# Ten instead of seven down chunks of a float32 MLP with seven block products, and what was rearranged for it

## Chip, cores, metric

One core of a Trainium2 chip. The metric is the device time of one execution in microseconds (us), the median of several runs.

## The reference, cut to what matters

One decoder layer in float32: 256 tokens, model width 2048, 16 heads of 128 (8 of forgetting attention, 8 of dilated attention), then a squared-ReLU MLP of width 8192.

```python
proj = rms_norm(x, norm1_g) @ w_in                 # 2048 x 6152
... two groups of heads, each with an output norm
x = x + mixed @ w_out                              # 2048 x 2048
h = rms_norm(x, norm2_g)
x = x + jnp.square(jax.nn.relu(h @ w_mlp_in)) @ w_mlp_out   # 2048 x 8192, 8192 x 2048
return rms_norm(x, final_norm_g)
```

## The kernel before, in words

**Precision.** Every float32 weight or activation is split into a high and a low part in float32r (ACT copies the high part, `whi`; DVE subtracts it, `wlo`), and a product is three matmuls: high x high, high x low, low x high. A matmul takes 128 weight columns or tokens and streams 256 or 512 columns.

**Tiling.** Each projection is cut into chunks of 512 output columns and each chunk into steps of two k-tiles (2 x 128 rows of the weight). The weights come from HBM in raw tiles of four k-tiles (1 MB, `raw`, L177, on SP's queue); a raw tile serves two steps. A raw tile is free for a new load when its last split has run (`spent`); there are 4 (`wraw`), and `load_more` keeps 4 in use.

**The MLP** runs in four rounds. In each, four up chunks (`u`) give 2048 of the 8192 hidden features, squared, as `hT` (in `big_hi`, `big_lo`), and four down chunks (`d`) add their share to the residual `xs`. A plain step is 24 matmuls of 256 columns: `turned_product` (L414) for up, `product` (L398) for down.

**Seven-product chunks.** Seven down chunks (`seven`, L140) use a scheme of Strassen's kind over 2 x 2 blocks (two token halves, two column halves, two k halves): seven block products instead of eight. It needs sums of weight blocks (`both`, made by DVE at L207, L222, L223 in `split_seven`) and sums of activation blocks (`mix_hi`, `mix_lo`, made by `mix_activations` and `split_mixed`). Such a chunk has four units of one raw tile, and a unit has four steps: "near" (12 matmuls), "first" (6), "odd" (12), "even" (12), in `seven_products` (L460); a plain step of another chunk is put between "odd" and "even". Its four PSUM banks are those of the names "sc" and "tr"; `drain_seven` adds them into `xs` in four parts. Before, the first down chunk of a round runs its units inside the up chunks of the next round, and the second with the steps of the third.

**Order.** The program is written out by hand: `steps` lists the steps in PE's order; the split of a step is called some steps ahead of its products (five step tiles of `whi` and `wlo` are live at a time, and one of `fhi`, `flo` for "first"); other work (drains, norms) is put in by `at(slot, ...)`, two slots a step, and runs on its engine's queue in the order of the calls. `drain_u` reads an up chunk's two PSUM banks (ACT: ReLU, square, high part; DVE: low part), all in the slot that ends the chunk; `mix_activations` and `split_mixed` follow 2 and 4 slots later.

**PSUM.** Eight banks by name: four "acc" for plain chunks, two "sc" and two "tr" for attention and the seven-product chunks, each name a ring of its own.

Of the kernel before, what the change touches and what calls it, by code (L numbers as in the profile page):

```python
# [19 lines left out]
P = 128  # L20
# [4 lines left out]
NH = 8  # L25
# [50 lines left out]
def kernel(  # L76
# [31 lines left out]
    psum = ctx.enter_context(tc.tile_pool(name="psum", bufs=2, space=PSUM))  # L108
# [5 lines left out]


# [24 lines left out]
    seven = {index["d", (r, c)] for r in range(ROUNDS) for c in range(2) if c or r < ROUNDS - 1}  # L140
# [4 lines left out]
    def mixed(ci, unit, behind):  # L145
        b, a, t13, t24 = ((ci, 2 * unit, sub) for sub in ("near", "first", "odd", "even"))
        return [b, a, t13, behind[0], t24] + behind[1:]

    for r in range(ROUNDS):
        for c in range(4):  # L150
            mine = plain(index["u", (r, c)])
            steps += mine[:4] + (mixed(index["d", (r - 1, 0)], c, mine[4:]) if r else mine[4:])
        late = [index["d", (r, c)] for c in range(4)]
        steps += plain(late[3 if r < ROUNDS - 1 else 0])
        for unit in range(4):
            steps += mixed(late[1], unit, plain(late[2])[2 * unit:2 * unit + 2])
        if r == ROUNDS - 1:
            steps += plain(late[3])
# [6 lines left out]
    def load(i):  # L165
        if i >= len(steps) or steps[i][1] % 2 or (steps[i][0], steps[i][1] // 2) in raws:
            return
        ci, s, _ = steps[i]
        _, _, w, r0, c0, cols, _ = chunks[ci]
        t = wraw.tile([P, 4, CW + NH], F32, name="raw")  # L170
# [15 lines left out]
    ring = [0]  # L186
# [9 lines left out]
    late_tiles, late_forms, sums_of = {}, ExitStack(), {}  # L196

    def halves(t):
        return t.rearrange("p k (f c) -> p f k c", f=2)

    def split_seven(i):
        ci, s, sub = steps[i]
        t = raws[ci, s // 2][:, :, :CW]
        half = CW // 2
        if sub == "near":
            both = sums_of[ci, s] = late_tiles["pool"].tile([P, 2, CW], F32, name="both")
            nc.vector.tensor_tensor(halves(both), t[:, :, half:].rearrange("p (f k) c -> p f k c", f=2),  # L207
                                    halves(t[:, :2]), op=ALU.subtract)
        if sub == "first":
            hi, lo = (late_tiles["pool"].tile([P, CW + LINE], F32R, name=n)[:, b:b + CW]  # L210
                      for n, b in (("fhi", NEAR), ("flo", NEAR)))
            src = t[:, :2, :half]
        else:
            hi, lo = part_tiles(i, 2 * CW, NEAR, NEAR)
            src = t[:, 2:] if sub == "near" else sums_of[ci, s]
        hi, lo = (a.rearrange("p (k c) -> p k c", k=2) for a in (hi, lo))
        splits[i] = (hi, lo)
        nc.scalar.activation(hi, src, AF.Copy)  # L218
        nc.vector.tensor_tensor(lo, src, hi.bitcast(F32), op=ALU.subtract)  # L219
        if sub == "odd":  # L220
            a, b = src[:, :, :half], src[:, :, half:]
            nc.vector.tensor_tensor(a, t[:, 2:, half:], a, op=ALU.subtract)  # L222
            nc.vector.tensor_tensor(b, t[:, 2:, :half], a, op=ALU.subtract)  # L223
            spent.add((ci, s // 2))
# [87 lines left out]
    pw = psum.tile([P, 512], F32, name="sc")  # L312
# [6 lines left out]
    def gains(k0, k1):  # L319
        p = psum.tile([P, 512], F32, name="tr")  # L320
# [22 lines left out]
    def to_features(kt0, gain, n=2):  # L343

        p = psum.tile([P, 512], F32, name="tr")
# [4 lines left out]
        for j in range(n):  # L350
            kt = kt0 + j
            split_psum(aT_hi[:, kt, :], aT_lo[:, kt, :], p[:, j * SEQ:(j + 1) * SEQ], gT[:, gain + kt:gain + kt + 1],
                       gain == kt == 0)

# [46 lines left out]
    def turned_product(ci, i, j, kt, kts):  # L401


        if kt == 0:
            accs[ci] = [psum.tile([P, CW], F32, name="acc", bufs=4) for _ in range(2)]
# [12 lines left out]
    def products(i, j):  # L418
# [10 lines left out]
        if kt == 0:  # L429
            accs[ci] = [psum.tile([P, CW], F32, name="acc", bufs=4) for _ in range(TB)]  # L430
# [7 lines left out]
    def seven_products(i, j):  # L438

        ci, s, sub = steps[i]  # L440
        if ci not in accs:
            accs[ci] = [psum.tile([P, CW], F32, name=n) for n in ("sc", "sc", "tr", "tr")]
# [7 lines left out]
            "odd": ((two_, half, m, k2, upper), (four, 0, m, k1, upper)),  # L450
            "even": ((three, half, m, k1, lower), (two_, 0, h, k2, upper)),
# [3 lines left out]
        for n, (bank, c0, (ah, al), k, tokens) in enumerate(todo):  # L455
            acc = bank[:, c0:c0 + half]
            fresh = begin and (bank, sub) in ((one_, "near"), (three, "first"), (two_, "odd"), (four, "odd")) and (
# [5 lines left out]
    def gated_products(ci, i, j, kt, kts, a):  # L463

        if kt == 0:
            accs[ci] = [psum.tile([P, 512], F32, name=n, bufs=k) for n, k in (("acc", 4), ("acc", 4), ("sc", 2))]
# [48 lines left out]
    def gate_sums():  # L515
        m = psum.tile([P, 512], F32, name="tr")
# [19 lines left out]
    def rel_row():  # L536
        p = psum.tile([P, 512], F32, name="sc")
# [52 lines left out]
    def first_norm_rows():  # L590
        d = diagonal.pop()
        square = d[:, SEQ:SEQ + P]
        p = psum.tile([P, 512], F32, name="tr")
# [29 lines left out]
    def scores(g, h):  # L623
# [5 lines left out]
        bank = psum.tile([P, 512], F32, name="sc")  # L629
# [40 lines left out]
    def turn_probs(g, h):  # L670
        pr = probs.pop((g, h))
        p = psum.tile([P, 512], F32, name="tr")
# [9 lines left out]
    def values(g, h):  # L682
# [4 lines left out]
        y = psum.tile([P, 512], F32, name="sc")  # L687
# [19 lines left out]
    def group_norm(kind):  # L707
        p = psum.tile([P, 512], F32, name="tr")
# [8 lines left out]
    rstd2sq = few.tile([P, TB], F32, name="rstd2sq")  # L717
# [10 lines left out]
    def second_norm():  # L728
        nc.vector.tensor_reduce(ssq2s, ssq2, axis=mybir.AxisListType.X, op=ALU.add)
        rsqrt(rstd2, ssq2s, D_MODEL)  # L730
        nc.vector.tensor_tensor(rstd2sq, rstd2, rstd2, op=ALU.mult)

# [3 lines left out]
    def drain_u(r, c, ci):  # L736

        hT_hi, hT_lo = squares()
        acc = accs.pop(ci)
        kept[c] = []  # L740
        for half in range(2):
            h = two.tile([P, CW], F32, name="nat")
            nc.scalar.activation(h, acc[half], AF.Relu)
            nc.scalar.activation(h, h, AF.Square)
            k0 = 4 * c + 2 * half
            split_psum(
                hT_hi[:, k0:k0 + 2, :].rearrange("p k s -> p (k s)"),
                hT_lo[:, k0:k0 + 2, :].rearrange("p k s -> p (k s)"), h,
            )
            kept[c].append(h.rearrange("p (k s) -> p k s", k=2))  # L750

    kept = {}

    def mix_activations(c):

        a, b = kept[c]
        (a11, a21), (a12, a22) = ((x[:, :, :P], x[:, :, P:]) for x in (a, b))
        nc.vector.tensor_tensor(a22, a21, a22, op=ALU.add)
        nc.vector.tensor_tensor(a21, a11, a21, op=ALU.subtract)
        nc.vector.tensor_tensor(a11, a22, a11, op=ALU.subtract)  # L760
        nc.vector.tensor_tensor(a12, a12, a11, op=ALU.subtract)

    def split_mixed(c):
        for half, x in enumerate(kept.pop(c)):
            k0 = 4 * c + 2 * half
            split_psum(mix_hi[:, k0:k0 + 2, :], mix_lo[:, k0:k0 + 2, :], x)
# [12 lines left out]
    def drain_d(r, c, ci):  # L779
        for t in range(TB):  # L780
            add_down(accs[ci][t], t, slice(c * CW, (c + 1) * CW), c if r == ROUNDS - 1 else None)

    def drain_seven(r, c, ci, part):
# [4 lines left out]
        def add(t, cs, acc):  # L788
            xc = xs[:, t, cs]
            if len(acc.shape) > 2:  # L790
# [244 lines left out]
```

## Time and profile before

| | |
|---|---|
| median of 3 runs | 1082.13 us (1082.01 to 1082.14) |
| the profiled execution: its time, its span | 1082.24 us, 1080.4 us |
| PE busy | 1069.3 us (99%), 8693 matmuls |
| DVE, ACT, POOL busy | 800.2 (74%), 604.4 (56%), 27.9 us (3%) |
| mean granted TensorE clock | 0.997 |
| loads of the MLP weights | 128 of 1 MB, 5.5 and 5.0 us from issue to landing |
| HBM read and written over the span | 193 GB/s |

PE is TensorE's matmuls, PEld its weight loads, DVE VectorE, ACT ScalarE, POOL GpSimd, SP the engine whose queue issues most DMAs. A group row reads: line, engine, operation, out<-in, shapes, count | busy us, mean ns of one | idle us of the engine just before them, and what released it. A timeline row reads: start us, duration us, engine, line, operation, out<-in, count, [idle before <-releaser].

### The profile page before, as it was taken

How to read it: one execution, taken by the hardware profiler on the slowest of the kernel's cores; microseconds unless marked ns; L12 is line 12 of the kernel's file. 1: busy time of each engine (PE TensorE's matmuls, PEld its weight loads, DVE VectorE, ACT ScalarE, POOL GpSimd, SP SyncE). 2: the span in 40 equal slices, each digit the busy share in tenths (PEclk: the TensorE clock that was granted, in tenths of full speed). 3: DMA queues.
4: the chain of work that ended last, by engine and by line, in shares of the span. 5: the costliest groups of instructions: out<-in, count | busy, mean ns of one | idle time of the engine just before them, and what ended most of it. 6: DMA issues, size and time to landing. Idle time of an engine off the chain costs nothing.

```text
span 1080.4 us, 20584 instructions
## 1 busy us (share of the span) xinstructions
PE 1069.3 (99%) x8693; PEld 1037.8 (96%) x8693; DVE 800.2 (74%) x1076; ACT 604.4 (56%) x821; POOL 27.9 (3%) x42
## 2 busy tenths in 40 slices
PE   9999999999999999999999999999999999999996
PEld 7999899998988899999999999999999999999996
DVE  6666756667577666559887788987778886778886
ACT  6555535545455555565556665556665555666561
POOL 0010200000001000000000000000000000000000
PEclk9999999999999999999999999999999999999998
DMA  9765464555554557654676654665656566556652
GB/s 323 238 226 165 157 197 154 195 159 172 201 172 163 185 166 221 201 196 161 219 217 194 202 209 166 201 208 178 199 202 223 196 197 193 196 195 217 211 198 79
DMA packets 105401, 209.38 MB, mean 194 GB/s; under 512 B 3971, under 2 KB 5084, under 8 KB 105180
## 3 DMA queue, kind: packets, MB, share of 16 engines
q1 hardware_dynamic: 104412, 206.59, 57.8%
q8 instruction: 68, 1.11, 0.4%
q0 software_dynamic: 304, 1.06, 0.3%
q10 hardware_dynamic: 592, 0.40, 0.1%
q14 instruction: 25, 0.20, 0.1%
HBM read 205.93 MB, written 2.11 MB: 193 GB/s over the span
## 4 chain that ended last, share of the span: by engine, by line
PE 99%; DMA 0%; DVE 0%; POOL 0%; ACTq 0%; DVEq 0%; issue 0%
PE acc L414 48%; PE acc L398 34%; PE sc L460 7%; PE tr L460 5%; PE tr L349 1%; PE sc L690 1%; PE sc L398 1%; PE sc L646 1%; PE tr L674 0%; DMA xs<-in_x_dram 0%; PE sc L642 0%; PE sc L692 0%; PE sc L636 0%; PE sc L640 0%; DVE xs L858 0%; PE sc L694 0%
## 5 line engine op out<-in xcount | busy, mean ns | idle before, releaser
L253 DVE TENSOR_TENSOR wlo<-raw,whi 128x1024 fp32r<-128x1024 f32 (+2 forms) x327 | 394.3, 1221 | 151.6 <-ACT whi L252 148.4
L252 ACT ACTIVATE whi<-raw 128x1024 fp32r<-128x1024 f32 (+2 forms) x328 | 339.5, 1050 | 218.5 <-PE acc L414 129.8
L414 PE MATMUL acc<-aT_hi,whi 128*128 128x256 f32 x1536 | 425.4, 277 | 0.0
L414 PE MATMUL acc<-aT_hi,wlo 128*128 128x256 f32 x1536 | 423.8, 276 | 0.0
L414 PE MATMUL acc<-aT_lo,whi 128*128 128x256 f32 x1536 | 423.7, 276 | 0.0
L414 PEld LDWEIGHTS acc<-aT_hi,whi 128*128 128x128 f32 x1536 | 288.2, 188 | 1.1 <-issue 0.9
L414 PEld LDWEIGHTS acc<-aT_lo,whi 128*128 128x128 f32 x1536 | 288.2, 188 | 0.1
L414 PEld LDWEIGHTS acc<-aT_hi,wlo 128*128 128x128 f32 x1536 | 288.1, 188 | 0.1
L398 PE MATMUL acc<-whi,big_hi 128*128 128x256 f32 (+1 forms) x680 | 202.8, 298 | 0.0
L398 PE MATMUL acc<-wlo,big_hi 128*128 128x256 f32 (+1 forms) x680 | 202.3, 297 | 0.0
L398 PE MATMUL acc<-whi,big_lo 128*128 128x256 f32 (+1 forms) x680 | 202.2, 297 | 0.0
L398 PEld LDWEIGHTS acc<-wlo,big_hi 128*128 128x128 f32 x680 | 127.6, 188 | 5.1
L398 PEld LDWEIGHTS acc<-whi,big_lo 128*128 128x128 f32 x680 | 127.7, 188 | 4.7
L398 PEld LDWEIGHTS acc<-whi,big_hi 128*128 128x128 f32 x680 | 127.6, 188 | 4.7
L218 ACT ACTIVATE whi<-both 128x1024 fp32r<-128x1024 f32 x56 | 59.8, 1067 | 55.1 <-DVE both L223 26.2
L219 DVE TENSOR_TENSOR wlo<-both,whi 128x1024 fp32r<-128x1024 f32 x56 | 68.3, 1220 | 6.7 <-ACT whi L218 5.8
L336 DVE TENSOR_TENSOR big_lo<-nat,big_hi 128x512 fp32r<-128x512 f32 x32 | 22.2, 693 | 43.7 <-ACT big_hi L335 43.7
L398 PE MATMUL acc<-whi,aT_hi 128*128 128x512 f32 (+1 forms) x144 | 51.7, 359 | 0.0
L398 PE MATMUL acc<-whi,aT_lo 128*128 128x512 f32 (+1 forms) x144 | 51.0, 354 | 0.0
L398 PE MATMUL acc<-wlo,aT_hi 128*128 128x512 f32 (+1 forms) x144 | 51.0, 354 | 0.0
L335 ACT ACTIVATE mix_hi<-nat 128x512 fp32r<-128x512 f32 x32 | 18.5, 625 | 29.9 <-DVE nat L760 29.9
L218 ACT ACTIVATE whi<-raw 128x1024 fp32r<-128x1024 f32 x28 | 29.6, 1058 | 9.4 <-PE acc L398 6.4
(212 smaller groups left out, 1356.7 us busy)
## 6 DMA issues: line engine op xcount, KB each, us to landing
raw<-in_w_mlp_in_dram SPq DMA_DIRECT2D x64, 1024.0 KB, 5.5
raw<-in_w_mlp_out_dram SPq DMA_DIRECT2D x64, 1024.0 KB, 5.0
raw<-in_w_in_dram SPq DMA_DIRECT2D x42, 1024.0 KB, 5.2
raw<-in_w_out_dram SPq DMA_DIRECT2D x16, 1024.0 KB, 5.0
raw<-in_w_in_dram SPq DMA_DIRECT2D x4, 1040.0 KB, 8.7
xs<-in_x_dram SPq DMA_DIRECT2D x3, 512.0 KB, 9.5
raw<-in_w_in_dram SPq DMA_DIRECT2D x2, 512.0 KB, 5.3
big_lo<-rel_d POOLq DMA_DIRECT2D x1, 1024.0 KB, 7.8
```

The costliest lines, as they stand in the source:

```text
L218: nc.scalar.activation(hi, src, AF.Copy)
L219: nc.vector.tensor_tensor(lo, src, hi.bitcast(F32), op=ALU.subtract)
L252: nc.scalar.activation(hi[:, :, c:c + step], t[:, :, c:c + step], AF.Copy)
L253: nc.vector.tensor_tensor(lo, t, hi.bitcast(F32), op=ALU.subtract)
L335: nc.scalar.activation(hi, src, AF.Copy)
L336: nc.vector.tensor_tensor(lo, src, hi.bitcast(F32), op=ALU.subtract)
L349: nc.tensor.transpose(p[:, j * SEQ + t * P:j * SEQ + (t + 1) * P], xs[:, t, c:c + P], ident)
L398: nc.tensor.matmul(acc, x, part[:, j, cols], start=go and n == 0, stop=end and n == 2, skip_group_check=True)
L414: nc.tensor.matmul(acc, w[:, j, b * P:(b + 1) * P], a[:, kt, :], start=kt == 0 and b % 2 == 0 and n == 0, stop=kt == kts - 1 and n == 2, s ...
L460: nc.tensor.matmul(acc, a[:, k, tokens], w[:, j, n * half:(n + 1) * half], start=fresh and x == 0, stop=s == KT // 2 - 2 and j == 1 and x ...
L646: nc.tensor.matmul(s[:, c0:c1], q[:, a, h, rows], k[:, b, h, keys], start=False, stop=n == 2, skip_group_check=True)
L690: nc.tensor.matmul(y[:, :SEQ], v[:, 0, dims], p[:, m, :SEQ], start=n == 0, stop=False, skip_group_check=True)
```

## The change

- **More seven-product chunks.** Ten of the 16 down chunks: the first three (A, B, C) of rounds 0 to 2, and the second of the last round.
- **Their order.** Units are dealt over the whole round by patterns: `2 A0 3 A1 1` means two plain steps, unit 0 of A, three plain steps, unit 1 of A, one plain step; each unit takes one more plain step inside. A runs in the last up chunk and the fourth down chunk, B from there into the next round's first up chunk, C in its second and third. The drain of a round's first up chunk (from the second round on) is put 14 slots later, since C's first unit still reads the features that it overwrites.
- **Unit sums.** The tile `both` is gone: sums are made in place in the raw tile. The first is made by a DMA from POOL's queue that adds half of the first two k-tiles of the weight (256 KB, rows of 1 KB) onto the other half of the raw tile; three adds or subtracts of 512 elements a partition follow on DVE. Signs in `mix_activations`, `seven_products` and `drain_seven` change to match (a negated scale `rstd2neg`).
- **Tiles.** A fifth raw tile (`raw5`). "first" takes one of the five step tiles, half used. A raw tile of a unit is spent at "even" instead of "odd".
- **PSUM.** One ring of eight banks in the MLP: the bank that has been free longest is taken (`take_bank`), and a drain gives its banks back as it reads them (`give_back`); a seven-product chunk takes a bank when a product first needs it.
- **Drains.** `drain_u`, its low parts (`rest_u`), the mixes and their splits are dealt out over ten slots, half by half; `drain_seven` runs in four consecutive slots.

```diff
-    seven = {index["d", (r, c)] for r in range(ROUNDS) for c in range(2) if c or r < ROUNDS - 1}
+    seven = [index["d", (r, c)] for r in range(ROUNDS) for c in range(3) if r < ROUNDS - 1 or c == 1]
...
+    def weave(ci, r, pattern):
+        rest = plain(ci)
+        for token in pattern.split():
+            if token.isdigit():
+                steps.extend(rest[:int(token)])
+                del rest[:int(token)]
+                continue
+            of = index["d", (r - 1 if token.endswith("-") else r, "ABC".index(token[0]))]
+            b, a, t13, t24 = ((of, 2 * int(token[1]), sub) for sub in ("near", "first", "odd", "even"))
+            steps.extend([b, a, t13] + rest[:1] + [t24])
+            del rest[:1]
+
+    behind = ["2 B1- 1 B2- 1 B3- 1", "2 C0- 2 C1- 2", "2 C2- 2 C3- 2"]
+    begun = [["8", "8", "8", "2 A0 3 A1 1"]] + [behind + ["2 A0 3 A1 1"]] * 2 + [behind + ["8"]]
     for r in range(ROUNDS):
...
+        for c, pattern in enumerate(begun[r]):
+            weave(index["u", (r, c)], r, pattern)
+        if r < ROUNDS - 1:
+            weave(index["d", (r, 3)], r, "1 A2 2 A3 2 B0")
+        else:
+            weave(index["d", (r, 0)], r, "2 B0 2 B1 2")
+            weave(index["d", (r, 2)], r, "1 B2 2 B3 3")
+            steps += plain(index["d", (r, 3)])
...
+        if steps[i][2]:
+            nc.gpsimd.dma_start(t[:, :2, CW // 2:CW], src[:, :2, :CW // 2], accum_op=ALU.add)
...
-            if len(raws) - len(spent) >= 4:
+            if len(raws) - len(spent) >= (5 if late_tiles else 4):
...
     def split_seven(i):
...
+        left, right = slice(0, half), slice(half, CW)
+        size = half if sub == "first" else CW
+        hi, lo = (a.rearrange("p (k c) -> p k c", k=2) for a in part_tiles(i, 2 * size, NEAR, NEAR))
+        splits[i] = (hi, lo)
+        x = {"near": t[:, 2:], "first": t[:, :2, left]}.get(sub, t[:, :, right])
...
+        nc.scalar.activation(hi, x, AF.Copy)
+        nc.vector.tensor_tensor(lo, x, hi.bitcast(F32), op=ALU.subtract)
+        first, second = t[:, :2, right], t[:, 2:, right]
         if sub == "near":
+            nc.vector.tensor_tensor(second, second, first, op=ALU.add)
+        elif sub == "odd":
+            nc.vector.tensor_tensor(first, second, t[:, :2, left], op=ALU.subtract)
+            nc.vector.tensor_tensor(second, second, t[:, 2:, left], op=ALU.add)
+        elif sub == "even":
             spent.add((ci, s // 2))
...
+        if s == j == 0:
+            held = accs.setdefault(ci, [None] * 4)
+            for n in {"near": (0,), "first": (2,), "odd": (1,), "even": (3,)}[sub]:
+                held[n] = take_bank("sc")
...
+    def drain_u(c, ci, half):
+        h = two.tile([P, CW], F32, name="nat")
+        kept[c] = kept[c] + [h] if half else [h]
+        nc.scalar.activation(h, accs[ci][half], AF.Relu)
+        give_back(accs[ci][half])
+        nc.scalar.activation(h, h, AF.Square)
+        nc.scalar.activation(both_squares(c, half)[0], h, AF.Copy)
+
+    def rest_u(c, half):
+        hi, lo = both_squares(c, half)
+        nc.vector.tensor_tensor(lo, kept[c][half], hi.bitcast(F32), op=ALU.subtract)
...
     def drain_seven(r, c, ci, part):
...
         if part == 0:
...
+            nc.scalar.activation(s[:, 1], four[:, left], AF.Copy)
             nc.scalar.activation(s[:, 0], three[:, left], AF.Copy)
             add(0, cs, one_)
+            give_back(four, one_)
         elif part == 1:
+            nc.vector.tensor_tensor(rest, rest, late_tiles["copies"][:, 0], op=ALU.subtract)
             add(0, cs, three)
             add(0, slice(cs.start + half, cs.stop), two_[:, right])
         elif part == 2:
+            nc.vector.tensor_tensor(rest, rest, late_tiles["copies"][:, 1], op=ALU.subtract)
             add(1, cs, two_)
+            give_back(two_)
         else:
-            add(1, cs, rest[:, None, :].to_broadcast([P, 2, half]))
+            add(1, slice(cs.start, cs.start + half), rest, rstd2neg)
+            add(1, slice(cs.start + half, cs.stop), rest)
+            give_back(three)
             accs.pop(ci)
...
         elif what == "u":
-            at(e, drain_u, *key, ci)
-            at(e + 2, mix_activations, key[1])
-            at(e + 4, split_mixed, key[1])
+            if key[0] and not key[1]:
+                e += 14
+            for half in range(2):
+                at(e + half, drain_u, key[1], ci, half)
+                at(e + 1 + half, rest_u, key[1], half)
+                at(e + 3 + half, mix_activations, key[1], half)
+                at(e + 6 + half, split_mixed, key[1], half, False)
+                at(e + 8 + half, split_mixed, key[1], half, True)
         elif ci in seven:
             for part in range(4):
-                at(e + 1 + 2 * part, drain_seven, *key, ci, part)
+                at(e + 2 + part, drain_seven, *key, ci, part)
...
     def free_tiles(i):
-        live = [steps[n][2] for n in range(i, done + 2) if not (steps[n][0] == len(chunks) - 1 and steps[n][1] < 3)]
-        return len([n for n in live if n != "first"]) <= 5 and live.count("first") <= 1
+        return len([n for n in range(i, done + 2) if steps[n][0] < len(chunks) - 1 or steps[n][1] > 2]) <= 5
...
     for i in range(final):
         if i == mlp_start:
+            unused_banks += turns["acc"][:2] + turns["sc"] + turns["tr"] + turns["acc"][2:]
...
+            late5.tile([P, 4, CW], F32, name="raw5")
```

More of the change, by code (lines that the diff above doesn't have):

```diff
@@ L113, with take_bank, give_back @@
     ctx.enter_context(tc.manual_schedule())
+    turns = {"acc": [0, 1, 2, 3], "sc": [4, 5], "tr": [6, 7]}
+    unused_banks, number = [], {}
+    def take_bank(kind):
+        if late_tiles:
+            n = unused_banks.pop(0)
+        else:
+            n = turns[kind].pop(0)
+            turns[kind].append(n)
+        t = psum.tile([P, CW], F32, name=f"bank{n}")
+        number[id(t)] = n
+        return t
+    def give_back(*tiles):
+        if late_tiles:
+            unused_banks.extend(number[id(t)] for t in tiles)
     chunks = []
@@ L204, in split_seven @@
         half = CW // 2
-        if sub == "near":
[L206 to L223, printed above, removed]
+        left, right = slice(0, half), slice(half, CW)
[3 more added lines that the diff above has]
+        x = {"near": t[:, 2:], "first": t[:, :2, left]}.get(sub, t[:, :, right])
+        if sub in ("odd", "even"):
+            hi, lo = (a.rearrange("p k (f c) -> p f k c", f=2) for a in (hi, lo))
+            x = x.rearrange("p (f k) c -> p f k c", f=2)
+        nc.scalar.activation(hi, x, AF.Copy)
+        nc.vector.tensor_tensor(lo, x, hi.bitcast(F32), op=ALU.subtract)
+        first, second = t[:, :2, right], t[:, 2:, right]
+        if sub == "near":
+            nc.vector.tensor_tensor(second, second, first, op=ALU.add)
[3 more added lines that the diff above has]
+        elif sub == "even":
             spent.add((ci, s // 2))
@@ L404, in turned_product @@
         if kt == 0:
-            accs[ci] = [psum.tile([P, CW], F32, name="acc", bufs=4) for _ in range(2)]
+            accs[ci] = [take_bank("acc") for _ in range(2)]
         hi, lo = splits[i]
@@ L429, in products @@
         if kt == 0:
-            accs[ci] = [psum.tile([P, CW], F32, name="acc", bufs=4) for _ in range(TB)]
+            accs[ci] = [take_bank("acc") for _ in range(TB)]
         go, end = kt == 0, kt == kts - 1
@@ L449, in seven_products @@
             "first": ((three, 0, h, k1, lower),),
-            "odd": ((two_, half, m, k2, upper), (four, 0, m, k1, upper)),
-            "even": ((three, half, m, k1, lower), (two_, 0, h, k2, upper)),
+            "odd": ((two_, half, m, k2, upper), (three, half, m, k1, lower)),
+            "even": ((four, 0, m, k1, upper), (two_, 0, h, k2, upper)),
         }[sub]
@@ L456, in seven_products @@
             acc = bank[:, c0:c0 + half]
-            fresh = begin and (bank, sub) in ((one_, "near"), (three, "first"), (two_, "odd"), (four, "odd")) and (
+            fresh = begin and (bank, sub) in ((one_, "near"), (three, "first"), (two_, "odd"), (four, "even")) and (
                 bank is not one_ or n == 0)
@@ L731, in second_norm @@
         nc.vector.tensor_tensor(rstd2sq, rstd2, rstd2, op=ALU.mult)
+        nc.vector.tensor_scalar(rstd2neg, rstd2sq, -1.0, None, op0=ALU.mult)
     def squares():
         return rows_at(big_hi, BIG_HI), rows_at(big_lo, BIG_LO)
[L736 to L750, printed above, removed]
@@ L768, with split_mixed @@
+    def split_mixed(c, half, rest):
+        k = slice(4 * c + 2 * half, 4 * c + 2 * half + 2)
+        hi, lo, x = mix_hi[:, k, :], mix_lo[:, k, :], kept[c][half].rearrange("p (k s) -> p k s", k=2)
+        if rest:
+            nc.vector.tensor_tensor(lo, x, hi.bitcast(F32), op=ALU.subtract)
+        else:
+            nc.scalar.activation(hi, x, AF.Copy)
     ssq3 = few.tile([P, TB, 5], F32, name="ssq3")
```

94 lines of the change are left out of this document (42 added, 52 removed).

## Prediction

> **What bounds the kernel now.** I read the page first (busy shares, clock, chain), then the windows of the MLP, then the groups, then the timelines of the tightest places.
>
> ```profile
> span 1080.4 us, 20584 instructions
> PE 1069.3 (99%) x8693; PEld 1037.8 (96%) x8693; DVE 800.2 (74%) x1076; ACT 604.4 (56%) x821; POOL 27.9 (3%) x42
> PE 99%; DMA 0%; DVE 0%; POOL 0%; ACTq 0%; DVEq 0%; issue 0%
> ```
>
> PE is never without work, and the chain of waits is PE from end to end. The MLP, where all of the change lies, in the view by windows (PE, PEld, DVE, ACT, POOL busy with their counts; clock; DMA share; GB/s):
>
> ```profile
> 394.20:1071.60 677.40, 677.40 (x5978) 677.23 (x5976) 533.45 (x620) 392.87 (x474) 2.03 (x3) 1.00 0.60 196
> 831.90:872.70 40.80, 40.80 (x363) 40.80 (x362) 35.55 (x38) 22.02 (x23) 0.00 (x0) 1.00 0.61 204
> ```
>
> 677.40 us over 5978 matmuls is 0.1133 us each, at full clock, with no gap. The timeline of PE shows the same step from start to start, across the border between a unit of a seven-product chunk (L460) and a plain step (L414), 0.12 and 0.11 us:
>
> ```profile
> 806.15 0.28 PE L460 MATMUL tr<-whi,mix_lo 128*128 128x256 f32 x1
> 806.27 0.28 PE L414 MATMUL acc<-aT_hi,whi 128*128 128x256 f32 x1
> 806.38 0.28 PE L414 MATMUL acc<-aT_lo,whi 128*128 128x256 f32 x1
> ```
>
> So a matmul fewer is worth 0.1133 us, and the only question is whether its feeders (DVE, ACT, loads) keep up.
>
> **What the change removes from PE.** A plain down chunk is 16 k-tiles x 2 token halves x 2 column halves x 3 terms = 192 matmuls of 256 columns. A seven-product chunk is 4 units x (12 + 6 + 12 + 12) = 168, of the same kind. Seven such chunks become ten: 3 x 24 = 72 matmuls fewer (5976 to 5904), 72 x 0.1133 = 8.16 us. Nothing else is taken from PE or added to it; the sign changes and the new order of steps leave the matmul count alone.
>
> **What it adds on DVE.** Prices, from the groups (mean ns) of the MLP window:
>
> ```profile
> L253 DVE TENSOR_TENSOR wlo<-raw,whi 128x1024 fp32r<-128x1024 f32 x194 | 234.3, 1222 | 85.0 <-ACT whi L252 83.0
> L207 DVE TENSOR_TENSOR both<-raw 128x1024 f32<-128x1024 f32 x28 | 34.1, 1217 | 0.0
> L219 DVE TENSOR_TENSOR flo<-raw,fhi 128x512 fp32r<-128x512 f32 x28 | 19.1, 683 | 0.0
> L222 DVE TENSOR_TENSOR both<-raw,both 128x512 f32<-128x512 f32 x28 | 19.4, 692 | 1.0
> L336 DVE TENSOR_TENSOR big_lo<-nat,big_hi 128x512 fp32r<-128x512 f32 x32 | 22.2, 693 | 43.7 <-ACT big_hi L335 43.7
> L792 DVE SCALAR_TENSOR_TENSOR xs<-tr,rstd2sq,xs 128x512 f32<-128x512 f32 x14 | 10.4, 745 | 0.0
> L792 DVE SCALAR_TENSOR_TENSOR xs<-sc,rstd2sq,xs 128x256 f32<-128x256 f32 x7 | 3.4, 484 | 0.2
> L801 DVE TENSOR_TENSOR tr<-tr,copies 128x256 f32<-128x256 f32 x7 | 3.0, 425 | 0.0
> L758 DVE TENSOR_TENSOR nat<-nat 128x256 f32<-128x256 f32 x16 | 6.7, 417 | 0.0
> ```
>
> A unit before: one 1217 (the sums), three low parts of 1222, one of 683, two of 692: 6.95 us. After: the 1217 goes, the first sum is the transfer's, and three 512-wide sums in place stand instead of two: 3.67 + 0.68 + 2.08 = 6.43 us. Twelve units more take 77.2 and give back 24 plain splits of 1.222 (29.3); 28 units save 0.52 each (14.7); three seven-chunk drains instead of plain ones: a new one is two of 425, three of 745, one of 742-745 less (the last add of 512 becomes two of 484), in all 2 x 0.425 + 3 x 0.745 + 3 x 0.484 = 4.54 against two of 0.745, so +3.05 each (9.1), and the seven old ones +0.22 each (1.6). Sum: +43.9, DVE 533 to 577 of 669 us, from 79% to 86%. ACT's part of it:
>
> ```profile
> L252 ACT ACTIVATE whi<-raw 128x1024 fp32r<-128x1024 f32 x315 | 328.4, 1058 | 211.3 <-PE acc L414 129.8 <-PE acc L398 56.7 <-PE tr L460 9.0
> L218 ACT ACTIVATE fhi<-raw 128x512 fp32r<-128x512 f32 x28 | 17.3, 616 | 0.0
> L799 ACT ACTIVATE copies<-tr 128x256 f32<-128x256 f32 x7 | 2.6, 369 | 0.0
> ```
>
> 12 x (3 x 1.06 + 0.62) - 24 x 1.06 and three pairs of copies, 22 us more: 415, 62%. It does not bound.
>
> A mean hides the densest stretch. That is the last down chunk of rounds 0 to 2: 8 plain steps with three units (A2, A3, B0), 318 matmuls, 36.0 us of PE. Durations overstate DVE there, because its instructions overlap; one unit of before in the timeline gives the true steps:
>
> ```profile
> 842.76 1.22 DVE L207 TENSOR_TENSOR both<-raw 128x1024 f32<-128x1024 f32 x1
> 843.90 1.22 DVE L219 TENSOR_TENSOR wlo<-raw,whi 128x1024 fp32r<-128x1024 f32 x1
> 845.03 0.69 DVE L219 TENSOR_TENSOR flo<-raw,fhi 128x512 fp32r<-128x512 f32 x1
> 845.63 1.22 DVE L219 TENSOR_TENSOR wlo<-both,whi 128x1024 fp32r<-128x1024 f32 x1
> 846.89 0.69 DVE L222 TENSOR_TENSOR both<-raw,both 128x512 f32<-128x512 f32 x1
> 847.61 0.69 DVE L223 TENSOR_TENSOR both<-raw,both 128x512 f32<-128x512 f32 x1
> 848.22 1.22 DVE L253 TENSOR_TENSOR wlo<-raw,whi 128x1024 fp32r<-128x1024 f32 x1
> 849.52 1.23 DVE L219 TENSOR_TENSOR wlo<-both,whi 128x1024 fp32r<-128x1024 f32 x1
> ```
>
> 1.14 for 1024 wide, 0.60 for 512, 0.72 where the next reads the result. A unit of after is 3 x 1.14 + 0.60 + 0.61 + 0.72 + 0.61 = 5.96. The stretch: 8 x 1.14 + 3 x 5.96 = 27.0, the drain of the up chunk before it some 4.0 (four low parts of 0.60, four half-width mixes of about 0.4), the drain of A some 4.3: 35.3 of 36.0 us, 98%. Before, the densest was the 831.90 window, 35.55 of 40.80 (87%). The stretches on either side are at about 88% (31.3 us of PE) and 77% (36.0), so a lag is not carried on.
>
> **Does the lag reach PE?** What counts is when a low part ends against the start of its matmuls. Before, the tightest place comes after each up drain, where DVE waits in order for the chain on ACT:
>
> ```profile
> 791.51 0.60 ACT L743 ACTIVATE nat<-acc 128x512 f32<-128x512 f32 x1 [1.09 <-PE acc L414]
> 793.34 0.58 ACT L743 ACTIVATE nat<-acc 128x512 f32<-128x512 f32 x1
> 795.16 1.05 ACT L218 ACTIVATE whi<-raw 128x1024 fp32r<-128x1024 f32 x1
> 804.27 1.22 DVE L253 TENSOR_TENSOR wlo<-raw,whi 128x1024 fp32r<-128x1024 f32 x1
> ```
>
> That low part ends at 805.49 and its matmuls start at 806.27 (quoted above): 0.78 us to spare, nine times in the kernel, and no wait of PE. After, the drain is dealt out: 1.83 us of ACT a half, with a split between the halves. I count from PE's start of the first step behind an up chunk (time 0), with four steps split ahead. In the dense stretch: ACT ends half 0 at 1.4, the high part of the plain step inside A2 at 2.4, half 1 at 4.2, that of A2's "even" at 5.2; DVE then ends its low part at 6.4 (PE wants it at 8.84), the mixes at 8.2, the next plain low part at 9.3 (PE: 10.2), the one behind it at 10.6 (12.92). Least room 0.9 us. In the last up chunk of rounds 1 and 2, where the drain of C comes on top (0.8 us of it after time 0): "odd" with its two sums ends at 4.95, the up chunk's low parts at 7.0, the plain step's low part at 8.1 (PE: 8.84), the mixes at 9.9, "even" at 11.0 (11.56). Least room 0.5 us. So I put the waits at 0 to 0.3 us in all. If ACT and DVE together run 1.3 us later than counted, these five places (three and two) lose 0.4 to 0.8 us each: 2 to 4 us, the upper end.
>
> The banks: by the new order a bank is taken at the earliest 66 matmuls (7.5 us) after the drain that frees it is called (C0's "odd", a new round's first up chunk). DVE ran within 6 us of its calls in the places worked out above, so cost 0, with about 1 us a place if that cover is gone. The steps behind a drain are on DVE's own queue, counted already.
>
> **The transfer on POOL's queue.** It is new: 40 of 256 KB, in rows of 1 KB, adding in SBUF, each waiting on POOL for its own load; POOL has nothing else in the MLP until the end (2.03 us of work). DVE's first in-place sum waits for it, and everything behind that on DVE. The nearest rows are the two POOL transfers of the attention part (12 KB and 1 MB, the latter in 1 KB rows) and the loads:
>
> ```profile
> L544 POOL DMA_DIRECT2D big_lo<-rel_d x1: 977/977/977, 69.2 to 69.2; - x1
> DMA to landing us min/median/max: 1.9/4.9/7.8
> big_lo<-rel_d POOLq DMA_DIRECT2D x1, 1024.0 KB, 7.8
> raw<-in_w_mlp_out_dram SPq DMA_DIRECT2D x64, 1024.0 KB, 5.0
> ```
>
> 1.9 for 12 KB and 7.8 for 1 MB: between them 3.3 us for 256 KB, which I take, being nearest in size and run length. Below, 1.9; above, 7.8, or 15.6 if reading and adding to the target doubled it. Room: in a dense stretch two raw tiles (one unit, two plain steps: 90 matmuls) last 10.2 us, so five raw tiles last 25.5; a tile is in use from its first to its last split, 842.76 to 850.75 above, 8.0 us; 17.5 are left for load and transfer, 5.0 + 3.3 = 8.3. In the order's tightest place the load is called 144 matmuls (16.3 us) ahead of the split, and about 2.5 are lost until the tile is free: 13.8. Cost 0, also at 7.8. DMA carries 10.5 MB more over a share of 0.60: 0.03 to 0.06 more. The fifth raw tile is what pays for it, since now the tile is kept until "even".
>
> **Sum.** The profiled execution took 1082.24 us (span 1080.4); 1082.24 - 8.16 = 1074.08. The median of the runs shown, 1082.13, lies 0.11 below. With 0.1 for waits: 1074.1 us.
>
> **Rivals.** (1) *DVE is late in the dense stretches.* For it: 98% and 0.5 to 0.9 us of room; against: before ran with 0.78 and lost nothing, and the lag is worked off in the next stretch. With 0.48 us lost in each of the five places, 2.4 us: 1076.5. (2) *The transfer is late, the other side.* Each unit then waits for it on DVE, and loads wait for tiles: the cycle of five tiles is 8.0 + 5.0 + transfer instead of 25.5. At 15.6 it is 28.6, 12% more in the six densest stretches (216 us): +26 us, 1100. It eats the gain from 3.8% of a cycle, 1.0 us over, a transfer of 13.5 us on. For it: no adding transfer is in the trace; against: 1 MB took 7.8. (3) *POOL's issue is held up by a busy DVE.* DVE's longest run without a gap is about the 8.0 us above; then 5.0 + 3.3 + 8.0 = 16.3, inside 17.5 but 2.5 over the tightest 13.8; a lag of 2.5 us on DVE, where the order leaves 0.5 to 0.9, costs 1 to 2 us in each of the three densest stretches: about 5 us, 1079. The L544 issue took 0.98 us with little DVE work around it, which leaves it open. [...] (4) *The gain does not show at all*, as waits of PE replace it: 1082; this needs 1.6 us lost in each of the five places, against 0.5 to 0.9 us of room in the count.
>
> **How the numbers follow.** Forecast 0.70, rival 1 0.14, rival 2 0.08, rival 3 0.05, rival 4 0.03. The range goes from 1073.6 (no wait, and the sum against the median, with the scatter of the runs) to 1077.5 (rival 1); rivals 2 to 4 are left out. A difference under 0.2% (2.2 us) is about what this measurement cannot tell from none. Faster by more: forecast, rival 1, part of rival 3: 0.88; same 0.03; slower 0.09.
>
> **What would show it.** Right: 5904 matmuls in the MLP over about 669 us at 0.1133 us, PE at 99%, DVE busy near 577 us there, POOL transfers landing in 2 to 8 us, the gap ahead of DVE's in-place sums near zero. Wrong: PE idle released by DVE low parts in the last down chunk of rounds 0 to 2 or in the last up chunk of rounds 1 and 2 (rival 1); DVE idle released by the transfer, in every unit (2) or with a long POOL issue (3); PE waiting for a drain at a unit's first matmul (banks).

## Result and the profile after

| | before | after |
|---|---|---|
| time, median (range) | 1082.07 us (1081.90 to 1082.14) | 1074.74 us (1073.73 to 1075.67), 4 runs |
| ratio, 95% interval | | 0.9926 [0.9914, 0.9938] |
| the profiled execution: time, span | 1082.24, 1080.4 us | 1075.40, 1073.6 us |
| MLP's matmuls, first to last start | 5976 in 677.16 us | 5904 in 669.26 us |
| first matmul of the MLP starts at | 394.19 us | 395.45 us |

The page of after (busy time and share of each engine; the DMA queue of POOL; issues, size and median time to landing):

```profile
span 1073.6 us, 20818 instructions
PE 1062.7 (99%) x8621; PEld 1030.9 (96%) x8621; DVE 840.9 (78%) x1162; ACT 618.0 (58%) x851; POOL 76.1 (7%) x82
q0 software_dynamic: 11184, 11.55, 6.8%
raw<-in_w_mlp_out_dram SPq DMA_DIRECT2D x64, 1024.0 KB, 6.8
raw<-in_w_mlp_out_dram POOLq DMA_DIRECT2D x40, 256.0 KB, 4.6
```

PE has 72 matmuls fewer (8693 to 8621) and stays at 99%. The view by windows of after: the MLP, and the last down chunk of round 2 with its three units, which the prediction named as the densest stretch (PE, PEld, DVE, ACT, POOL busy; clock; DMA share; GB/s):

```profile
395.40:1064.90 669.50, 669.50 (x5906) 669.28 (x5905) 574.09 (x706) 406.75 (x504) 50.24 (x43) 1.00 0.68 212
823.90:859.94 36.04, 36.04 (x321) 36.04 (x319) 33.38 (x43) 23.55 (x30) 4.78 (x4) 1.00 0.74 219
```

No gap of PE is shown, though DVE went from 533 to 574 us. What DVE waited for at the first in-place sum (L250: us in all, times, longest), and how long the adding transfers (L213) took:

```profile
DVE raw L250 <- DMA raw<-in_w_mlp_out_dram: 2.9, 2, 1.6
...
DMA to landing us min/median/max: 4.2/4.6/9.0
```

38 of the 40 transfers had landed when DVE came to them, by 7.1 us at the median over all 40. Two had not, and PE lost a little behind each: 0.05 us in the last up chunk of round 2 (at 804.4 us), and 0.21 in the final round (at 1017.9), where a low part came 0.14 us after PE had reached its step.

One run of `twice3` (1306.29 us) fell in a slower state of the chip and is left out of the median given for it below.

**The profiled execution's account.** Predicted 1074.08; measured 1075.40. Of the 1.32 us, 0.27 are in the MLP: 669.26 against 5904 steps of 0.11333 us (669.00), 0.26 of them at these two places. 1.26 lie before the MLP, in the first ten microseconds: the trace's clock records have PE at full clock from 5.69 us in before, from 9.14 us in after. The rest (-0.21) is in the tail and around the span. The clock's change is seen in the timeline, where three idle products of 512 columns (L316 in before, L347 in after) took 0.81 and 1.49 us:

```profile
6.54 0.81 PE L316 MATMUL sc<-nat 128*128 128x512 bf16 x3
```

```profile
6.75 1.49 PE L347 MATMUL bank<-nat 128*128 128x512 bf16 x3
```

From matmul 300 on (40.87 and 42.13 us) the two executions run in step until the MLP. The times of both kernels fall into two such groups (below), so this is not the change's doing.

### The profile page after: what moved, and what is told of

The parts are those of the page before. It is cut to its first block, busy times and chain, and to the rows that moved or that the text cites. A ratio compares the mean times of both kernels' runs of the same rounds, so it can differ in the third digit from the quotient of the medians.

```text
span 1073.6 us, 20818 instructions
## 1 busy us (share of the span) xinstructions
PE 1062.7 (99%) x8621; PEld 1030.9 (96%) x8621; DVE 840.9 (78%) x1162; ACT 618.0 (58%) x851; POOL 76.1 (7%) x82
## 3 DMA queue, kind: packets, MB, share of 16 engines
q1 hardware_dynamic: 104412, 206.59, 57.3%
## 4 chain that ended last, share of the span: by engine, by line
PE 99%; DMA 0%; DVE 0%; POOL 0%; ACTq 0%; DVEq 0%; issue 0%
PE bank L446 49%; PE bank L430 29%; PE bank L494 18%; PE bank L380 1%; PE bank L724 1%; PE bank L680 1%; PE bank L708 0%; DMA xs<-in_x_dram 0%; PE bank L676 0%; PE bank L726 0%; PE bank L670 0%; PE bank L674 0%; PE bank L347 0%; DVE xs L902 0%; PE bank L728 0%; PE bank L572 0%
## 5 line engine op out<-in xcount | busy, mean ns | idle before, releaser
L446 PE MATMUL bank<-aT_hi,whi 128*128 128x256 f32 x1536 | 426.1, 278 | 0.0
L446 PE MATMUL bank<-aT_lo,whi 128*128 128x256 f32 x1536 | 423.8, 276 | 0.0
L446 PE MATMUL bank<-aT_hi,wlo 128*128 128x256 f32 x1536 | 423.7, 276 | 0.0
L446 PEld LDWEIGHTS bank<-aT_hi,whi 128*128 128x128 f32 x1536 | 288.7, 188 | 1.2 <-issue 0.6
L446 PEld LDWEIGHTS bank<-aT_lo,whi 128*128 128x128 f32 x1536 | 288.4, 188 | 0.1
L446 PEld LDWEIGHTS bank<-aT_hi,wlo 128*128 128x128 f32 x1536 | 288.1, 188 | 0.0
L246 ACT ACTIVATE whi<-raw 128x1024 fp32r<-128x1024 f32 (+1 forms) x160 | 150.9, 951 | 149.8 <-PE bank L446 55.4
L247 DVE TENSOR_TENSOR wlo<-raw,whi 128x1024 fp32r<-128x1024 f32 (+1 forms) x160 | 173.7, 1087 | 47.9 <-ACT whi L246 46.6
L430 PE MATMUL bank<-whi,big_hi 128*128 128x256 f32 (+1 forms) x488 | 149.8, 307 | 0.0
L430 PE MATMUL bank<-wlo,big_hi 128*128 128x256 f32 (+1 forms) x488 | 149.4, 306 | 0.0
L213 POOL DMA_DIRECT2D raw<-in_w_mlp_out_dram x40 | 48.2, 1205 | 559.2 <-DMA raw<-in_w_mlp_out_dram 242.5
```

The costliest lines, as they stand in the source:

```text
L213: nc.gpsimd.dma_start(t[:, :2, CW // 2:CW], src[:, :2, :CW // 2], accum_op=ALU.add)
L246: nc.scalar.activation(hi, x, AF.Copy)
L247: nc.vector.tensor_tensor(lo, x, hi.bitcast(F32), op=ALU.subtract)
L430: nc.tensor.matmul(acc, x, part[:, j, cols], start=go and n == 0, stop=end and n == 2, skip_group_check=True)
L446: nc.tensor.matmul(acc, w[:, j, b * P:(b + 1) * P], a[:, kt, :], start=kt == 0 and b % 2 == 0 and n == 0, stop=kt == kts - 1 and n == 2, s ...
```

## Experiments

Two theories stood against each other. A, the prediction's: PE never waits, the gain is the count of matmuls, and the order leaves DVE just enough room. B: the gain is partly eaten, and parts of the change are ballast or cost something. The runs on the start have theories of their own under these letters. The table gives the MLP's matmuls from first to last start, and from the window over them PE's idle time (its length less PE busy) and by how much PE busy exceeds 0.11333 us for each matmul in it (a lower clock, and short stops inside a recorded matmul; the window counts some matmuls that lie only partly in it, which makes this column about 0.25 us too small).

| kernel | time us | ratio to before | MLP us | PE idle | PE busy over its steps |
|---|---|---|---|---|---|
| after, unaltered (`again`) | 1074.28 | 0.9917 [0.9904, 0.9931] | 669.00 | 0 | 0 |
| nine chunks (`nine`) | 1076.60 | 0.9950 [0.9937, 0.9962] | 671.72 | 0 | 0 |
| before, drains dealt (`before_dealt`) | 1082.10 | 0.9999 [0.9990, 1.0008] | 677.16 | 0 | 0 |
| first sum on DVE (`sum_dve`) | 1075.25 | 0.9931 [0.9919, 0.9944] | 670.24 | 0.3 | 0.7 |
| banks apart (`fixed`) | 1079.24 | 0.9972 [0.9962, 0.9982] | 674.03 | 4.2 | 0.6 |
| drains in bulk (`bulk`) | 1089.35 | 1.0051 [1.0037, 1.0065] | 682.82 | 8.4 | 5.2 |
| four raw tiles (`raw4`) | 1115.03 | 1.0307 [1.0281, 1.0334] | 713.77 | 26.6 | 17.9 |
| transfer twice (`twice2`) | 1148.73 | 1.0605 [1.0548, 1.0663] | 750.15 | 49.1 | 31.8 |
| transfer three times (`twice3`) | 1250.73 | 1.155 [1.1521, 1.158] | 840.5 | 106.8 | 64.5 |

### The changed kernel again, and its start

`again` and `again2` are the changed kernel unaltered.

> The changed kernel once more, unaltered. Theory A (the gain is the 72 matmuls, and what lies between 1074.0 and the slower executions is the clock of the first 10 us): times fall in two groups, about 1073.7 to 1074.1 and 1075.3 to 1075.7, and this execution's profile shows the start of its group: the three idle products between the first transposes and the first weights take 0.8 us (full clock) or 1.5 us (half), and the MLP's 5904 matmuls take 669.1 to 669.5 us in both. Rival B (the spread is made in the MLP, by transfers that land late): the start is the same in all, and the MLP's matmuls take 669.3 us or over 670.5 us.

> The changed kernel unaltered, for its spread. Theory A (the moment at which the granted clock becomes full differs from run to run and sets two groups that lie 1.3 to 1.5 us apart): times at 1073.7 to 1074.6 and at 1075.3 to 1075.7, MLP's matmuls 669.0 to 669.3 us. Theory B (the two groups come of waits in the MLP): the slower profile has over 670 us there.

The MLP's view by windows in `again`:

```profile
394.40:1063.60 669.20, 669.20 (x5907) 669.15 (x5905) 574.30 (x706) 406.80 (x504) 50.24 (x43) 1.00 0.68 212
```

669.00 us from first to last start: 8.160 less than before, 72 x 0.11333 = 8.160. In `again2` it was 669.47. Of all 13 runs of the changed kernel, eight lie at 1073.7 to 1074.6 and five at 1075.4 to 1076.3 (two of these, in `again2`, above the 1075.7 that had been expected). In their three profiles PE's clock is full from 4.28 us (1074.17 us), 9.14 (1075.40) and 10.27 (1076.26, with 0.47 us of it lost in the MLP, at the same two places as in after). Before has the same pair of groups in the later runs, 1081.8 to 1082.7 and 1082.9 to 1084.0 with one run at 1085.3, though with only 0.3 us between the groups, and its variant with dealt drains shows the late start in its profile (10.15 us, 1083.80). The medians of the two groups lie 1.5 us apart in both kernels (1074.12 and 1075.67, 1081.92 and 1083.45).

More idle products ahead of the first real one, run twice:

```diff
-WARM, WARM2 = 8, 3
+WARM, WARM2 = 12, 3
```

> The changed kernel with 12 instead of 8 idle products ahead of the first transposes (1.7 us more of idle PE work at half clock, of which 1.1 us lie in a wait). Theory A: the full clock is there at 6 us in every execution, so all times are 1073.8 to 1074.4, with no second group. Rival B: two groups 1.6 us apart as before. Rival C (the moment of the clock does not depend on the work before it): two groups as well, with the idle products at 1.5 us in the slower.

> The changed kernel with 12 idle products ahead of the first real one instead of 8, a second time. Theory A (four idle products more let the clock become full before the real products begin): one group, all runs at or below 1074.6 us. Theory C (the moment is set by something that runs free of the kernel): two groups as in the changed kernel, some runs at 1075 us or above.

1074.17 us (0.9916 [0.9902, 0.9930]) and 1073.89 us (0.9923 [0.9911, 0.9936]); nine runs from 1073.67 to 1074.75, none in the upper group, where the unaltered kernel had five of 13. One run is 0.15 us above the line that theory A drew. The clock was full from 7.09 and 4.99 us, the MLP took 669.00 us in both. The timeline of `warm12b` shows PE waiting 0.23 us before the second transpose, the first that has to wait for its input, where after waited 1.07 us:

```profile
5.64 0.27 PE L380 MATMUL bank<-ident,xs 128*128 128x128 f32 x1
6.15 0.55 PE L380 MATMUL bank<-ident,xs 128*128 128x128 f32 x3 [0.23 <-DMA xs<-in_x_dram]
```

So the idle products fill a wait for the input and cost nothing, and the late start did not occur. By chance alone all five late runs of these 22 would fall on the unaltered kernel about once in 20 times, and beside `warm12` that kernel had no late run either (`again`), so that twelve products prevent the late start is likely but not shown; the gain, 0.4 us between the medians over all runs, is below what this measurement tells from none. What sets the moment, which goes from 4.28 to 10.27 us for one and the same kernel, is not shown.

### Nine chunks instead of ten

```diff
-if r < ROUNDS - 1 or c == 1]
+if (r < ROUNDS - 1 or c == 1) and (r, c) != (2, 2)]
-    ... + [behind + ["8"]]
+    ... + [behind[:1] + ["8"] * 3]
...
+            if r == 2:
+                steps += plain(index["d", (r, 2)])
...
-            if key[0] and not key[1]:
+            if key[0] in (1, 2) and not key[1]:
```

> Nine seven-product chunks of 16 instead of ten: the third down chunk of round 2 is made plain again (24 matmuls more, 8 dealt steps with their four transfers fewer). Theory A (PE never waits, so the time goes by the count of matmuls): 24 x 0.1133 = 2.72 us more than the change, MLP's matmuls 669.0 + 2.72 = 671.7 us, 1076.8 us in all, and the transfers left land in about 4.6 us as before. Theory B (the tenth chunk already costs waits, or its raw tiles and loads hold up others): less than 2.0 us more, at the least nothing (1074.1).

```profile
394.00:1065.80 671.80, 671.80 (x5930) 671.80 (x5929) 557.82 (x680) 401.67 (x494) 45.42 (x39) 1.00 0.68 210
```

671.72 us, 2.72 more than `again`: the 24 matmuls, to the hundredth. The tenth chunk is paid in full, its 16.5 us of DVE included (574.3 against 557.8). Theory B is out for the count of chunks.

### Drains: dealt out, or in bulk

```diff
             for half in range(2):
-                at(e + half, drain_u, key[1], ci, half)
-                at(e + 1 + half, rest_u, key[1], half)
-                at(e + 3 + half, mix_activations, key[1], half)
-                at(e + 6 + half, split_mixed, key[1], half, False)
-                at(e + 8 + half, split_mixed, key[1], half, True)
+                at(e, drain_u, key[1], ci, half)
+                at(e, rest_u, key[1], half)
+            ... mixes at e + 2, their splits at e + 4, both halves
```

> The up drains as before the change: both halves with their low parts in the slot that ends the chunk, the mixes two slots later, their splits four slots later; all else as changed. DVE then waits in its queue for ACT's chain (1.8 and 1.1 us in the trace of before) at each of 16 drains. Theory A (room of 0.0 to 0.9 us behind each drain of rounds 0 to 3 that units follow): 1 to 2.5 us lost at each of about ten drains, 1084 to 1099. Rival E (dealing them out was worth little, as before the change 0.78 us were left with the drain in one slot): under 2 us, 1074 to 1076.

`bulk` is slower than the kernel before. What PE waited for in its MLP:

```profile
PE bank L446 <- DVE wlo L284: 6.8, 9, 1.9
PE bank L430 <- DVE wlo L284: 1.5, 4, 0.8
```

```profile
395.80:1078.70 682.90, 674.55 (x5906) 671.99 (x5904) 574.36 (x706) 406.02 (x504) 50.23 (x43) 1.00 0.67 208
```

DVE's busy time is that of after (574); only its order differs. The two largest losses, 1.8 and 3.8 us, lie in the last up chunk of rounds 1 and 2, where the drain of C comes on top of the up drain. Of the 3.8 us, 1.6 come after PE's stop of 1.90 us, at half the clock:

```profile
812.31:815.72 3.41, 3.41 (x19) 3.41 (x18) 3.41 (x4) 2.98 (x4) 0.00 (x0) 0.50 0.35 77
```

In the kernel before the same dealing out (the up drains of after in before.py's order, nothing else) does nothing, as theory A had it:

> The kernel before with one part of the change alone: its up drains dealt out over ten places instead of four pieces of work in bulk; the seven chunks of before, their order and their banks stay. Theory A (before had room everywhere, so dealing out has nothing to shorten): no difference, 1082.1 us, MLP's matmuls 677.16 us. Theory B (dealing out has a gain or a price of its own, more instructions on DVE and ACT): at least 0.5 us off that, to either side.

```profile
395.80:1073.10 677.30, 677.30 (x5979) 677.30 (x5977) 535.01 (x620) 391.61 (x474) 2.03 (x3) 1.00 0.60 196
```

677.16 us again, ratio 0.9999. Dealing out is worth 13.8 us with ten chunks (1.6 of them this half clock) and nothing with seven.

### The first sum on DVE

```diff
-            nc.gpsimd.dma_start(t[:, :2, CW // 2:CW], src[:, :2, :CW // 2], accum_op=ALU.add)
...
+            nc.vector.tensor_tensor(first, first, t[:, :2, left], op=ALU.add)
```

> The first unit sum is made by DVE (one 512-wide add more a unit) instead of by the transfer. It adds 40 x 0.60 = 24 us to DVE, and the densest stretch goes from 98% to 37.1 of 36.0 us. Theory A (DVE's room was down to 0.0 to 0.9 us in about twenty places, so it is at its limit): the MLP gets 3 to 10 us longer, 1077 to 1084. Rival D (a lag of 0.6 us a unit is worked off before PE sees it; the transfer buys nothing): 1074 to 1075, as the changed kernel.

```profile
395.70:1066.00 670.30, 670.01 (x5906) 669.42 (x5904) 596.74 (x746) 404.56 (x504) 2.03 (x3) 1.00 0.58 196
```

DVE rises to 596.7 us, 89%, and the MLP loses 1.24 us: three stalls of 0.41 us, one behind each densest stretch, at the third plain step of the next round's first up chunk, which is none of the five places that the prediction named. There DVE has no gap and is simply late: PE's step waits from 869.92 for the low part that ends at 869.01 + 1.22 = 870.23 us.

```profile
869.01 1.22 DVE L283 TENSOR_TENSOR wlo<-raw,whi 128x1024 fp32r<-128x1024 f32 x1
...
869.92 0.28 PE L445 MATMUL bank<-aT_lo,whi 128*128 128x256 f32 x1
870.29 0.39 PE L445 MATMUL bank<-aT_hi,wlo 128*128 128x256 f32 x1
```

Theory A had expected more than twice this. The transfer takes 22 us of work from DVE and buys 1.2 us, since most of these 22 lay in slack.

### Banks

Plain chunks and seven-product chunks each get four of the eight banks, in place of the bank that has been free longest:

```diff
-            n = unused_banks.pop(0)
+            n = next(b for b in unused_banks if (b < 4) == (kind == "acc"))
+            unused_banks.remove(n)
```

> Banks are not taken by age from all eight: plain chunks keep four of their own, seven-product chunks the other four. Where one such chunk follows another, its first bank is then one whose drain was called only three slots (about 4 us) before, instead of 7.5 us and more. Theory A (DVE runs 4 to 6 us behind its calls behind a drain): 0.5 to 2 us of PE waiting at each of eight such places, 1077 to 1090. Rival (the drains run in time): 1074 to 1075.

PE's waits in `fixed`, one of the three in the timelines of DVE and PE, and the MLP by windows:

```profile
PE bank L495 <- DVE xs L833: 4.2, 3, 1.6
```

```profile
857.05 0.74 DVE L833 SCALAR_TENSOR_TENSOR xs<-bank,rstd2sq,xs 128x512 f32<-128x512 f32 x1
...
857.93 0.36 PE L495 MATMUL bank<-whi,mix_hi 128*128 128x256 f32 x1 [1.29 <-DVE xs L833]
```

```profile
394.00:1068.10 674.10, 669.92 (x5906) 669.42 (x5905) 574.59 (x706) 407.99 (x504) 50.24 (x43) 1.00 0.68 211
```

At the end of each densest stretch B starts where A has just ended; with banks of their own, B's product waits for DVE to read A's. 5.0 us in three places (eight had been expected), 1.6 to 1.9 each.

### Raw tiles, and the transfer made longer

Four raw tiles instead of five:

```diff
-            fifth = ring[1] % 5 == 0
+            fifth = False
...
-            if len(raws) - len(spent) >= (5 if late_tiles else 4):
+            if len(raws) - len(spent) >= 4:
```

> Four raw tiles instead of five. In a dense stretch four tiles last 20.4 us, 8.0 of them in use, so 12.4 are left for a load (6.8 us in the trace of after) and the transfer (4.6): 1.0 us of room there, and none where the order calls a load late. Theory A (the fifth tile pays for the transfer): DVE waits for transfers in many units, 1077 to 1090. Rival (loads run far enough ahead with four): 1074 to 1075.

```profile
395.70:1109.50 713.80, 687.17 (x5906) 681.43 (x5904) 573.90 (x706) 405.33 (x504) 50.24 (x43) 0.98 0.65 200
```

```profile
DVE raw L250 <- DMA raw<-in_w_mlp_out_dram: 57.4, 13, 7.5
```

The loads start one tile later, so the transfers do: landed ahead of the sum by 2.1 us at the median instead of 7.1, and DVE waits 57 us. The 44.8 us lost are more than theory A's upper end.

The transfer issued two or three times in a row (the block is then added once or twice too often):

```diff
-        if steps[i][2]:
+        for _ in range(2 if steps[i][2] else 0):      # 3 in the third kernel
             nc.gpsimd.dma_start(t[:, :2, CW // 2:CW], src[:, :2, :CW // 2], accum_op=ALU.add)
```

> Each transfer is issued twice, one behind the other (the second adds the same block again, so this kernel adds it one time too many). POOL waits for the first to land: 9.2 us instead of 4.6, with a load 16.0 us. Theory A (room of 17.5 us in a dense stretch, 13.8 in the tightest place): no wait in most units, 1074 to 1077. Rival (the transfer has no room to spare): 4.6 us late in each of 40 units less some lead, 1100 and over.

> Each transfer three times (the block is added two times too many): 13.9 us a unit on POOL, over the 13.5 us from which the prediction said that the gain is lost. In the densest stretches a unit comes every 10.2 us, so POOL itself falls behind there. Theory A: slower than before the change, 1090 to 1140. Rival (tiles and lead take up this too): under 1080.

The second waits for the first, so the pair takes 11.3 us from first issue to last landing (median), and three take 17.8. `twice2`, then `twice3`:

```profile
394.60:1144.90 750.30, 701.21 (x5907) 692.97 (x5905) 574.16 (x706) 404.12 (x504) 98.42 (x83) 0.96 0.71 203
```

```profile
DVE raw L250 <- DMA raw<-in_w_mlp_out_dram: 90.3, 14, 9.7
```

```profile
395.00:1236.00 841.00, 734.18 (x5909) 717.02 (x5909) 573.67 (x707) 403.53 (x504) 146.90 (x123) 0.93 0.71 194
```

```profile
DVE raw L250 <- DMA raw<-in_w_mlp_out_dram: 196.1, 26, 11.8
```

6.7 us more at the median cost 81 us in the MLP. Only 14 of 40 sums waited, but by up to 9.7 us (the pairs they waited for took 11.7 to 19.5), and 49 us of PE's time went idle. Another 32 us are PE's own steps grown longer: the granted clock falls (0.96, and 0.93 with three) after PE has stood still. The clock records of `twice2` have nine stretches at half clock in the MLP, 54.6 us together, which makes up to 27 of the 32. Theory A here, that 11 us would still be hidden, is wrong.

## Why the prediction was right, and where its steps were off

**The count (right).** 72 matmuls of 0.11333 us are 8.160 us, shown by `again` (-8.160) and, for one chunk, by `nine` (+2.72). The median, 1074.74, is 0.6 over the forecast because two of its four runs lie in the late group; the two of the early one took 1073.73 and 1074.07; over all 13 runs it is 1074.38. The prediction had no term for the start; it is 1.26 of the 1.32 us that its sum is off by in the profiled execution.

**DVE and ACT (right).** 574 and 407 us in the MLP for 577 and 415. The window over PE's densest stretch has DVE at 33.4 us of 36.0 (93%), but DVE splits ahead of PE, so this window does not hold the stretch's own work. That work (eight plain low parts, three units and the two drains) runs from 818.14 to 857.73 us:

```profile
818.14:857.73 39.59, 39.59 (x352) 39.59 (x351) 36.16 (x47) 25.63 (x32) 3.61 (x3) 1.00 0.77 235
```

It is 36.2 us, where the steps made 35.3 and PE's stretch is 36.0. DVE pays for it from its lead: the stretch's first low part is ready 4.55 us ahead of PE (819.35 for 823.90), its last 1.64 us (856.94 for 858.58). So the sum of steps was 2% too small, and DVE came in early enough for it.

**Room ahead of PE (right in the dense stretch, half right in the last up chunk).** The timeline of after, for the dense stretch's tightest place by the count, the plain step behind "even" of A2 (low part, then the step's first matmul), and for "even" in the last up chunk of round 2:

```profile
831.95 1.22 DVE L284 TENSOR_TENSOR wlo<-raw,whi 128x1024 fp32r<-128x1024 f32 x1
...
834.10 0.28 PE L430 MATMUL bank<-whi,big_hi 128*128 128x256 f32 x1
```

```profile
790.93 0.69 DVE L250 TENSOR_TENSOR raw<-raw 128x512 f32<-128x512 f32 x1 [1.29 <-DMA raw<-in_w_mlp_out_dram]
...
802.87 1.22 DVE L247 TENSOR_TENSOR wlo<-raw,whi 128x1024 fp32r<-128x1024 f32 x1
804.12 0.28 PE L494 MATMUL bank<-whi,mix_hi 128*128 128x256 f32 x1
```

834.10 - 833.17 = 0.93 us, predicted 0.9, and 0.92 in rounds 0 and 1. 804.12 - 804.09 = 0.03, predicted 0.5. In round 1 the same place has 0.48 in after, `again` and `again2`: the count of instructions was right. What it left out in round 2 is the late transfer twelve microseconds earlier: of its 1.29 us DVE had not yet made good 0.45. The other profiles of the changed kernel agree: there the room in round 2 is 0.37 us after a wait of 0.96 (`again`) and -0.10 after 1.43 (`again2`), where PE loses 0.17 us. So rival 1 came in a trace of itself, at one of its five places, and behind a late transfer. Elsewhere the room held; `sum_dve` adds 0.56 us of DVE work a unit and loses 0.41 us three times.

**The banks (right, with the cover named).** No wait in after; with the cover gone, 1.6 to 1.9 us in each of three places for "about 1 us a place".

**The transfer (right in effect, sizes wrong).** Landing 4.6 us at the median and 9.0 at most, taken as 3.3 with 7.8 above; the load of the same weights 6.8 us, taken as 5.0 from the kernel before. Not all of that comes of the transfers: in `sum_dve`, with the new order and none of them, the load takes 6.1.

```profile
raw<-in_w_mlp_out_dram SPq DMA_DIRECT2D x64, 1024.0 KB, 6.1
```

The step between the trace's two rows of 12 KB and 1 MB, which do not add to their target, is what failed in the transfer's size. The transfers share the 16 DMA engines with the loads (6.8% of the engines' span for POOL's queue, 57.3% for that of the loads): of after's 40, the 11 with no load issued between 3 us before and 5 us after their own issue took 4.2 us at the median and 5.1 at most; all of the longer ones had at least one load there. What slows one of them to 8 or 9 us is not settled: others with as many loads beside them took 4.3.

**Rival 2's price (wrong).** "A transfer of 13.5 us on" came from a cycle of five tiles, 25.5 us on average, though the prediction had the tight place's 13.8 us in the line above. The first of the two transfers that DVE waited for in after shows the sum at such a place (issue of the load, then of the transfer):

```profile
772.89 0.37 SPq L211 DMA_DIRECT2D raw<-in_w_mlp_out_dram  x1
...
782.00 1.20 POOL L213 DMA_DIRECT2D raw<-in_w_mlp_out_dram  x1 [18.60 <-DVE raw L253]
```

The row names DVE, which was done at 781.01; the last part of the load landed at 781.39. The transfer starts 9.1 us after the load's issue and takes 8.8, 17.9 us in all; DVE was ready for its sum 16.7 us after the load's issue (789.64). The other late one took 8.2. At a median of 11.3 us `twice2` is at 1148.7, where the cycle allowed no loss at all (0.6 us a cycle with the load at 6.8). Two terms were missing. A late transfer holds up everything behind it on DVE, which gives its tiles back later, so that the next loads start later too (argued from the order, not measured apart). And PE, having stood still, ran at half the clock for a time (the half-clock stretches of `twice2`, 54.6 us together). The chance of 0.08 was for a case nearer than it looked.

**"The fifth raw tile is what pays for it" (right, and large).** 44.8 us of MLP without it.

**Rival 3 (did not come).** POOL's issue took 1.20 us (1203 ns at the least and in the median, 1266 at most) beside a DVE at 86%, against 0.98 for the 1 MB transfer of before: no hold-up near the 8.0 us that the rival counted with.

## What to carry to other kernels

Where PE had no gap, a matmul removed was worth its step (72 of them 8.160 us, 0.11333 us each), as long as the feeder's work was dealt out so that no low part came late: the same busy time of DVE (574 us) gave 669 us dealt out and 683 us in bulk. Price a transfer that DVE waits for, with all its later work behind it, by the tightest place in the order and its longest landing (9.0 us here), not by an average cycle and its median (4.6). Rearrangements of this kind are to be judged together: dealing out, the fifth tile and banks by age are worth 13.8, 44.8 and 5.0 us with ten chunks, and dealing out alone was worth nothing with seven.

## What was not expected of the hardware

- The start of one and the same kernel falls into two groups about 1.5 us apart, by when the clock becomes full: at 4.3 to 5.7 us or at 9.1 to 10.3 in the profiles with eight idle products; four more, in a wait that is there anyway, gave 5.0 and 7.1.
- Standing still cost PE twice: in `raw4`, `twice2` and `twice3`, 0.6 to 0.7 us of slower steps came with each microsecond of idle time (17.9 to 26.6, 31.8 to 49.1, 64.5 to 106.8), but next to none in `fixed` (0.6 to 4.2). `bulk`'s stop of 1.90 us was followed by 3.41 us at half clock, which cost 1.6 us; the longest of `fixed`, 1.58 us, was not, as its slower steps come to 0.6 us in all. Why the one and not the other is not shown. The 3.41 us that hold each stop, `bulk` first:

```profile
808.90:812.31 3.41, 1.51 (x13) 1.40 (x12) 3.38 (x6) 3.01 (x5) 0.00 (x0) 1.00 0.00 0
```

```profile
687.31:690.72 3.41, 1.83 (x16) 1.66 (x15) 3.34 (x7) 2.66 (x3) 0.00 (x0) 1.00 0.58 155
```

- 40 adding transfers of 256 KB, 10.5 MB in all, came with loads of the same weights that landed in 6.8 us, at a DMA share of 0.68; the same kernel without them (`sum_dve`) has 6.1 and 0.58, the kernel before 5.0 and 0.60.
